# Eight modulation chunks of the first layer as scaled sums on ScalarE, GpSimd and VectorE instead of TensorE matmuls

## The chip, the core and the metric

The kernel runs on one core of a Trainium2 chip. The metric is the device time of one execution, in microseconds (us). Five engines of the core matter here, each with its own queue, worked off in order: TensorE (PE; its weight loads are listed apart as PEld), VectorE (DVE), ScalarE (ACT), GpSimd (POOL), and SyncE (SP), which here only issues DMA transfers. Engines wait for each other through semaphores. TensorE writes only to PSUM; tensors named z, zS, U, T, S and O lie there, all others used below in SBUF.

## The reference, cut to what matters

```python
def modulation(cond, w_ada, b_ada):
    m = jax.nn.silu(cond) @ w_ada + b_ada          # (1024) @ (1024, 6144)
    return [t[..., None, :] for t in jnp.split(m, 6, axis=-1)]
...
for i in range(DEPTH):                             # two layers
    sh1, sc1, g1, sh2, sc2, g2 = modulation(c, w_ada[i], b_ada[i])
    csh1, csc1, cg1, csh2, csc2, cg2 = modulation(c_ctx, w_ada[i], b_ada[i])
    h = modulate(rms_norm(x, norm1_g[i]), sh1, sc1)
    hc = modulate(rms_norm(ctx, norm1_g[i]), csh1, csc1)
    ...                                            # h @ w_in, mixers A, B and C
    x = x + g1 * (jnp.concatenate([out_a, out_b, out_c], axis=-1) @ w_out[i])
    x = x + g2 * conv_ffn(modulate(rms_norm(x, norm2_g[i]), sh2, sc2), ...)
    ...                                            # the same for ctx, unless last
```

There are 1024 latent tokens and 256 context tokens of width 1024, two layers. The modulation is a product of one vector per stream (latent with `c`, context with `c_ctx`) with a matrix of 1024 x 6144, cut by the kernel into 12 chunks of 512 columns. Chunks 0 to 3 (shift and scale of the first norm) are needed before the input projection. Chunks 4 to 11 (gate g1, then shift, scale and gate of the second half) are needed only from the output projection on.

## The kernel before

Tokens lie in 10 tiles of 128: tiles 0 to 7 latent, 8 and 9 context. The first layer normalises tiles in the order `al` = 8, 9, 0, 1, 2 and `be` = 3 to 7. `ipset` (L1042) runs the input projection block by block (`cb` 3, 2, 1, 0, each 512 columns), and for each block tile by tile in `inproj` (L415). One tile of one block is 24 matmuls of 128x128 on 128x512 (L132: three terms of high and low halves, eight slices of the depth). Behind them the tile's result `z` is copied by ScalarE to `zs` (L435), normed and rotated in `rms_rope` (L369: ScalarE squares, VectorE sums, GpSimd raises to the power -1/2 at L381, VectorE and GpSimd rotate at L382 to L394), transposed on TensorE (L400, PSUM tile `U`, one buffer) and written to DRAM. Weights come in units of 512 KB into a ring of three buffers (`raw` of pool `wr`), and are split into halves by ScalarE (L115) and VectorE (L109).

Between the projection blocks stand the differential attention `attn_c` (scores at L696 into `S`, running maximum at L496 on VectorE, exponent at L704 on ScalarE, mix at L710 on VectorE, transposes at L724, output at L729) and the window attention `attn_b` (L568 to L620, closing at L629 to L637). Then follow the output projection in `prep` (L130 with `oT`), the second norm, and the MLP.

The modulation chunks 4 to 11 are `modset` calls at the end of that list (`range(4, 8)` and `range(8, 12)` around the last `ipset`). `mod_chunk` (L134) loads a chunk as four quarters of 256 rows (512 KB each, into the same `raw` ring as the weights), multiplies each 128 rows by the padded condition columns `cpad` on TensorE (L143), both streams at once, copies the 512-wide result (L144), transposes it with four TensorE transposes (L147), and sums and adds the bias on VectorE (L149, L151). The second layer does its chunks in another manner, during the first layer's MLP: `mod_wide` (L153) scales the rows on ScalarE (L167, L170), adds them on GpSimd (L171), transposes within blocks of 32 on VectorE (L176), reduces (L177), and at the end `mod_sum` (L180) sums over the blocks with small matmuls (L187).

The order of instructions in each engine's queue is not that of the source. A scheduler sets it when the program is built, with the source order as priority, and lets later work go ahead where its inputs and buffers are ready. So the trace shows attention matmuls between the projection's, and the chunks between both.

Of the kernel before, what the change touches and what calls it, by code (L numbers as in the profile page):

```python
# [52 lines left out]
def trunk(ctx: ExitStack, tc: tile.TileContext, a: dict):  # L53
# [127 lines left out]

    def mod_sum(L, c0, c1, ns, mkps):

        ps = mkps()
        n = (c1 - c0) * 4 * ns
        for b in range(4):
            pe.matmul(ps[32 * b:32 * b + 32, 0:n], four, st["modr"][:, b, c0:c1, :, 0:ns].rearrange("p c m s -> p (c m) s"),  # L187
                      start=True, stop=True)
        dve.tensor_tensor(out=mods[:, L, 4 * c0:4 * c1, 0:ns], in0=ps[:, 0:n].rearrange("p (c s) -> p c s", s=ns),
                          in1=bcol[:, L, 4 * c0:4 * c1].unsqueeze(2).to_broadcast([P, 4 * (c1 - c0), ns]), op=ALU.add)  # L190
# [9 lines left out]
    def norm_front(src, mkps, mkbig, f=None, ss=None):  # L200

        ms = sm.tile([P, 2], F32, tag="nms", name="nms")
        if ss is None:
            sq = mkbig()
            act.activation(out=sq, in_=src, func=AF.Square)
            red = sm.tile([P, P], F32, tag="red", name="red", bufs=1)
            for w_ in (4, 2):
                dve.tensor_tensor(out=sq[:, 0:w_], in0=sq[:, 0:w_], in1=sq[:, w_:2 * w_], op=ALU.add)
            dve.tensor_tensor(out=red, in0=sq[:, 0], in1=sq[:, 1], op=ALU.add)
            ps = mkps()  # L210
            pe.transpose(ps[:, 0:P], red, ident)
# [5 lines left out]
        dg = sm.tile([P, P], F32, tag="dg", name="dg", bufs=2)  # L217
# [289 lines left out]
    def units_b(L, tiles, at, mkS, mkT, mkO):  # L507
# [11 lines left out]
        def unit(g):  # L519
# [76 lines left out]
            def outputs(hp, pp):  # L596
# [34 lines left out]
                ob = at.tile([P, 512], F32, tag="ob", name="ob", bufs=1)  # L631
                act.activation(out=ob[:np_], in_=po[:np_], func=AF.Copy)
                dve.tensor_tensor(out=ob[:np_], in0=bc[:np_], in1=ob[:np_], op=ALU.mult)
                st = at.tile([P, 2, 512], F32R, tag="stb", name="stb", bufs=1)
                st = [st[:, 0], st[:, 1]]
# [428 lines left out]
    ipset(0, al, (1,))  # L1064
# [206 lines left out]
```

## Time and profile before

| | before |
|---|---|
| median of three runs | 3282.14 us (3276.18 to 3285.51) |
| profiled execution | 3282.18 us |
| its span, first to last instruction | 3280.3 us |
| busy share PE, DVE, ACT, POOL | 94%, 71%, 53%, 27% |
| start of the output projection of the first layer | 469.6 us |
| start of its first MLP matmul | 601.6 us |

The work that the change touches lies in the first 605 us of the span. A busy engine is not an engine at its peak: a wait inside a matmul counts as busy. The trace lists one fp32 matmul of the source as two where it is done in two passes, as at L143 (128 in the trace for chunks 4 to 11) and L187. "PEclk" is the share of the TensorE clock that was granted.

### The profile page before, as it was taken

The page shows a single profiled execution, that of the slowest core. Times are in us where ns is not written, and L with a number is a line of the kernel's source. Part 1 is how long each engine was busy: PE and PEld are TensorE (multiplying, and loading weights), DVE is VectorE, ACT ScalarE, POOL GpSimd, SP SyncE. Part 2 cuts the span into 40 slices and gives each one's busy share as a digit, 9 for nine tenths or more (in the row PEclk, how much of TensorE's full clock was granted, in tenths as well). Part 3 has the DMA queues.
Part 4 walks back from the last instruction along what each step waited for, and adds up shares of the span by engine and source line. Part 5 has one row for each costly group of instructions (what it writes and reads, how often), then busy time and mean ns, then how long its engine had stood idle before and what let it go on. Part 6 is the DMA issues. An engine that isn't in the chain of part 4 may idle for free.

```text
span 3280.3 us, 54515 instructions
## 1 busy us (share of the span) xinstructions
PE 3072.3 (94%) x19503; PEld 2754.6 (84%) x19503; DVE 2330.4 (71%) x5306; ACT 1742.7 (53%) x3075; POOL 892.2 (27%) x1170
## 2 busy tenths in 40 slices
PE   6999988899999899999999899999898999999999
PEld 3777656798999898989999777777897799999998
DVE  4776765766878875878776678757786685666666
ACT  3554545656656653646444345567675564444443
POOL 1445301133223640128101144223240322231000
PEclk8999998899999999999999999999999999999999
DMA  8655796345543763378333656455754546434443
GB/s 265 193 161 173 205 273 165 91 125 144 135 120 100 232 178 113 103 209 242 93 106 108 173 132 175 139 166 141 180 147 131 134 114 204 122 101 137 138 119 104
DMA packets 754126, 499.52 MB, mean 152 GB/s; under 512 B 81480, under 2 KB 697792, under 8 KB 753856
## 3 DMA queue, kind: packets, MB, share of 16 engines
q1 hardware_dynamic: 753856, 496.03, 53.1%
q8 instruction: 155, 2.54, 0.3%
q14 instruction: 115, 0.94, 0.1%
HBM read 432.48 MB, written 63.44 MB: 151 GB/s over the span
## 4 chain that ended last, share of the span: by engine, by line
PE 64%; DVE 11%; DMA 8%; ACT 4%; POOL 3%; issue 3%; SPq 1%; ACTq 0%; POOLq 0%; DVEq 0%
PE z L130 32%; PE zS L130 11%; PE z L132 6%; PE O L620 2%; DVE wsp L109 2%; DMA raw<-in_w_up_dram 2%; DMA mraw<-in_w_ada_dram 2%; PE T L610 2%; PE O L729 2%; DVE ec L496 2%; PE S L696 1%; POOL mev L171 1%; POOL wsp L109 1%; PE zS L132 1%; PE T L724 1%
## 5 line engine op out<-in xcount | busy, mean ns | idle before, releaser
L130 PE MATMUL z<-h,wsp 128*128 128x386 f32 (+3 forms) x5280 | 872.1, 319 | 17.4 <-ACT wsp L115 5.7
L130 PEld LDWEIGHTS z<-h,wsp 128*128 128x128 f32 x5280 | 821.9, 190 | 31.6 <-issue 9.3
L115 ACT ACTIVATE wsp<-raw 128x1024 fp32r<-128x1024 f32 (+2 forms) x660 | 555.7, 845 | 423.7 <-PE z L130 185.2
L109 DVE TENSOR_TENSOR wsp<-raw,wsp 128x1024 fp32r<-128x1024 f32 (+2 forms) x516 | 562.6, 1092 | 108.2 <-ACT wsp L115 105.2
L130 PE MATMUL z<-g,wsp 128*128 128x386 f32 (+3 forms) x2640 | 457.0, 321 | 13.7 <-DVE t L862 4.7
L130 PEld LDWEIGHTS z<-g,wsp 128*128 128x128 f32 x2640 | 415.6, 190 | 28.3 <-issue 8.8
L132 PE MATMUL z<-wsp,h 128*128 128x512 f32 x1584 | 406.2, 403 | 16.6 <-ACT h L233 5.3
L109 POOL TENSOR_TENSOR wsp<-raw,wsp 128x128 fp32r<-128x128 f32 x528 | 258.5, 522 | 426.6 <-ACT wsp L115 358.4
L132 PEld LDWEIGHTS z<-wsp,h 128*128 128x128 f32 x1584 | 293.5, 192 | 83.3 <-ACT zs L435 6.4
L130 PE MATMUL zS<-h,wsp 128*128 128x386 f32 (+1 forms) x2112 | 333.4, 313 | 9.8 <-DVE wsp L109 3.4
L130 PEld LDWEIGHTS zS<-h,wsp 128*128 128x128 f32 x2112 | 318.0, 190 | 12.6 <-DVE wsp L109 4.2
L855 ACT ACTIVATE t<-z,cw 128x386 f32<-128x386 f32 (+3 forms) x220 | 137.9, 627 | 186.3 <-PE z L130 184.9
L859 DVE SCALAR_TENSOR_TENSOR t<-z,cw,t 128x255 f32<-128x255 f32 (+3 forms) x264 | 132.4, 502 | 145.2 <-ACT t L855 144.5
L704 ACT ACTIVATE ec<-ec,nmc 128x1280 f32<-128x1280 f32 (+1 forms) x144 | 182.3, 1266 | 72.8 <-DVE ec L496 70.7
L171 POOL TENSOR_TENSOR mev<-mev,mtr 128x512 f32<-128x512 f32 x112 | 175.7, 1582 | 122.6 <-ACT mtr L170 119.7
L496 DVE TENSOR_SCALAR_CACHE_REDUCE ec<-S,nmc 128x512 f32<-128x512 f32 (+1 forms) x256 | 173.5, 678 | 41.1 <-PE S L696 36.7
L130 PE MATMUL z<-oT,wsp 128*128 128x384 f32 (+2 forms) x1056 | 198.9, 337 | 3.9 <-DMA oT<-o_s 3.7
L887 DVE SCALAR_TENSOR_TENSOR xg<-z,mods,xg 128x384 f32<-128x384 f32 (+5 forms) x288 | 140.1, 501 | 85.4 <-PE z L130 84.2
L130 PE MATMUL zS<-g,wsp 128*128 128x386 f32 (+1 forms) x1056 | 182.8, 317 | 9.7 <-DVE wsp L109 3.0
L130 PEld LDWEIGHTS z<-oT,wsp 128*128 128x128 f32 x1056 | 178.3, 190 | 12.0 <-issue 4.3
L381 POOL TENSOR_TENSOR rs<-ss,cst 128x8 f32<-128x8 f32 (+1 forms) x76 | 115.5, 1520 | 225.7 <-DVE ss L379 146.1
L696 PE MATMUL S<-Kc,qc 128*128 128x512 f32 (+1 forms) x400 | 143.6, 401 | 35.0 <-DVE ec L496 27.2
(248 smaller groups left out, 4678.6 us busy)
## 6 DMA issues: line engine op xcount, KB each, us to landing
raw<-in_w_up_dram SPq DMA_DIRECT2D x264, 512.0 KB
mraw<-in_w_ada_dram SPq DMA_DIRECT2D x96, 512.0 KB
raw<-in_w_down_dram SPq DMA_DIRECT2D x192, 256.0 KB
Kc<-qk_s SPq DMA_DIRECT2D x96, 320.0 KB
raw<-in_w_in_dram SPq DMA_DIRECT2D x52, 512.0 KB
raw<-in_w_out_dram SPq DMA_DIRECT2D x48, 512.0 KB
raw<-in_w_down_dram SPq DMA_DIRECT2D x104, 192.0 KB
qk_s<-st SPq DMA_DIRECT2D x18, 512.0 KB
```

The lines of the kernel that those rows point to most:

```text
L109: eng.tensor_tensor(out=lo, in0=src, in1=hi.bitcast(F32), op=ALU.subtract)
L115: act.activation(out=hl[:, 0], in_=raw, func=AF.Copy)
L130: pe.matmul(ps, w(i, k), h(j, k), start=s, stop=e)
L132: pe.matmul(ps, h(i, k), w(j, k), start=s, stop=e)
L171: pool.tensor_tensor(out=acc[s], in0=acc[s], in1=pr, op=ALU.add)
L381: pool.tensor_tensor(out=rs[:, :ns], in0=ss[:, 1, :ns], in1=mhalf[:, :ns], op=ALU.pow)
L496: dve.tensor_scalar(out=neg, in0=s_ap, scalar1=-1.0, scalar2=init, op0=ALU.mult, op1=ALU.min, accum_out=acc)
L696: pe.matmul(S[:, b * w_:b * w_ + w_], q[:, m, ti * P:ti * P + P], K[m][:, o:o + w_], start=True, stop=True)
L704: act.activation(out=es[m][:, :nk], in_=es[m][:, :nk], func=AF.Exp, scale=-1.0, bias=acc[m], accum_out=l1[:, m, ti:ti + 1])
L855: act.activation(out=t[:, o:o + n], in_=ps[:, :n], func=AF.Identity, scale=cw[:, L, 1, ft:ft + 1], bias=cw[:, L, 3, ft:ft + 1])
L859: dve.scalar_tensor_tensor(out=t[:, o + b + 1:o + e], in0=ps[:, b:e - 1], scalar=cw[:, L, 0, ft:ft + 1], in1=t[:, o + b + 1:o + e], op0=AL ...
L887: dve.scalar_tensor_tensor(out=xs, in0=ps[:, b + o0:b + o1], scalar=mods[:, L, 40 + ct, s:s + 1], in1=xs, op0=ALU.mult, op1=ALU.add)
```

## The change

Chunks 4 to 11 of the first layer go through a new function `mod_mix`. A quarter is loaded as before. The latent stream (s = 0) is scaled on ScalarE into a temporary and added to its sum on GpSimd; the context stream (s = 1) is multiplied and added in one VectorE instruction. After the fourth quarter VectorE transposes and reduces both sums, four small matmuls sum over the blocks, and VectorE adds the bias. A quarter is called before each tile of the projection blocks (`between=modq`) and before each head of one attention call, 32 quarters in all, and the two `modset` calls go.

Three smaller edits free SBUF: the second norm's last VectorE addition writes into its input instead of a tile `red`; `dg` has one buffer instead of two; and `ob` of the window attention is the second half of the output tile `stb`, which GpSimd then overwrites in place. `prep_loads` makes `oT` before `xg`.

```diff
+    def mod_mix(L, ch, mkraw, mkacc, mktr, mkps):
+        acc = [mkacc() for _ in range(2)]
+        def quarter(j):
+            raw = mkraw()
+            sp.dma_start(out=raw, in_=a["w_ada"][L, j * 256:j * 256 + 256, ch * 512:ch * 512 + 512]
+                         .rearrange("(k p) c -> p k c", p=P))
+            for k in range(2):
+                c0, c1 = (cpad[:, 2 * j + k, s:s + 1] for s in range(2))
+                if j == 0 and k == 0:
+                    act.activation(out=acc[0], in_=raw[:, k], func=AF.Identity, scale=c0)
+                    dve.tensor_scalar(out=acc[1], in0=raw[:, k], scalar1=c1, scalar2=None, op0=ALU.mult)
+                else:
+                    pr = mktr()
+                    act.activation(out=pr, in_=raw[:, k], func=AF.Identity, scale=c0)
+                    pool.tensor_tensor(out=acc[0], in0=acc[0], in1=pr, op=ALU.add)
+                    dve.scalar_tensor_tensor(out=acc[1], in0=raw[:, k], scalar=c1, in1=acc[1], op0=ALU.mult,
+                                             op1=ALU.add)
+            if j < 3:
+                return
+            mr = sm.tile([P, 4, 4, 2], F32, tag="mr", name="mr", bufs=1)
+            for s in range(2):
+                tr = mktr()
+                dve.transpose(tr, acc[s])
+                dve.tensor_reduce(out=mr[:, :, :, s].rearrange("p b m -> p m b"),
+                                  in_=tr.rearrange("p (m b j) -> p m b j", b=4, j=32), axis=AX.X, op=ALU.add)
+            ps = mkps()
+            for b in range(4):
+                pe.matmul(ps[32 * b:32 * b + 32, 0:8], four, mr[:, b].rearrange("p m s -> p (m s)"), start=True, stop=True)
+            dve.tensor_tensor(out=mods[:, L, 4 * ch:4 * ch + 4], ...)
...
-            for w_ in (4, 2):
+            for w_ in (4, 2, 1):
                 dve.tensor_tensor(out=sq[:, 0:w_], in0=sq[:, 0:w_], in1=sq[:, w_:2 * w_], op=ALU.add)
-            dve.tensor_tensor(out=red, in0=sq[:, 0], in1=sq[:, 1], op=ALU.add)
...
-        dg = sm.tile([P, P], F32, tag="dg", name="dg", bufs=2)
+        dg = sm.tile([P, P], F32, tag="dg", name="dg", bufs=1)
...
+                st = at.tile([P, 2, 512], F32R, tag="stb", name="stb", bufs=1)
+                st = [st[:, 0], st[:, 1]]
+                ob = st[1].bitcast(F32)
...
-    ipset(0, al, (1,))
+    def modq(i=None):
+        n = mq["n"]
+        if n == 32:
+            return
+        if n % 4 == 0:
+            mq["q"] = mod_mix(0, 4 + n // 4, lambda: wr.tile([P, 2, 512], F32, tag="raw", name="mraw", bufs=3),
+                              lambda: wk.tile([P, 512], F32, tag="mev", name="mev", bufs=2),
+                              lambda: wk.tile([P, 512], F32, tag="sq", name="mtr", bufs=wb["sq"]), mkU)
+        mq["q"](n % 4)
+        mq["n"] += 1
+
+    ipset(0, al, (1,), between=modq)
...
-    ipset(0, al, (0,))
+    ipset(0, al, (0,), between=modq)
     st["wd"] = 1
-    ipset(0, be, (3, 2))
+    ipset(0, be, (3, 2), between=modq)
     for hd in range(4):
+        modq()
         attn_c(0, hd, [(0, 1)], at, mkS, mkT, mkO)
-    ipset(0, be, (1,))
-    modset(0, range(4, 8), wk, "kn", wr, "raw", 3, mkz, mkU)
-    ipset(0, be, (0,))
-    modset(0, range(8, 12), wk, "kn", wr, "raw", 3, mkz, mkU)
+    ipset(0, be, (1, 0), between=modq)
```

The temporaries take the tag `sq`, whose three buffers `rms_rope` uses too, and the quarters the `raw` ring of three.

How the built queues moved is shown at three places. In the changed program the lines are 33 higher from `norm_front` on and 34 higher inside the attention (L400 is L433, L696 is L730). On TensorE, in the differential attention of tiles 0 and 1 before (`zs` and `wst` belong to projection block 0 of tiles 3 to 7):

```order
L143 MATMUL z<-mraw,cpad 32x512 x2
L696 MATMUL S<-Kc,qc 128x512
L143 MATMUL z<-mraw,cpad 32x512 x2
L400 MATMUL U<-cst,zs 128x128 x2
L143 MATMUL z<-mraw,cpad 32x512 x2
L696 MATMUL S<-Kc,qc 128x512
L478 MATMUL U<-zs,wst 128x64 x4
```

and in the same attention in the changed program:

```order
L730 MATMUL S<-Kc,qc 128x512
L730 MATMUL S<-Kc,qc 128x256 x2
L132 MATMUL z<-wsp,h 128x512 x12
L730 MATMUL S<-Kc,qc 128x512
L211 MATMUL U<-mr,four 32x8 x4
L132 MATMUL z<-wsp,h 128x512 x44
L730 MATMUL S<-Kc,qc 128x512
```

The chunk's matmuls are gone there, four small ones stand for a whole chunk, and projection matmuls fill what lies between the scores.

On GpSimd, in projection block 1 of the first five tiles (q of the window attention), before:

```order
L381 TENSOR_TENSOR rs<-ss,cst 128x8
L390 TENSOR_TENSOR r_1489<-kn,tab 128x16x16 x2
L381 TENSOR_TENSOR rs<-ss,cst 128x8
L390 TENSOR_TENSOR r_1541<-kn,tab 128x16x16 x2
L381 TENSOR_TENSOR rs<-ss,cst 128x8
```

and now:

```order
L414 TENSOR_TENSOR rs<-ss,cst 128x8
L423 TENSOR_TENSOR r_1509<-kn,tab 128x16x16 x2
L198 TENSOR_TENSOR mev<-mev,mtr 128x512 x2
L414 TENSOR_TENSOR rs<-ss,cst 128x8
L423 TENSOR_TENSOR r_1571<-kn,tab 128x16x16 x2
L198 TENSOR_TENSOR mev<-mev,mtr 128x512 x2
```

Two additions of a quarter stand now between the two steps of one tile and those of the next.

On VectorE, in projection block 2 of tiles 3 to 7, the end of a chunk and the start of the next in the changed program (`stc` is attention output, `ko` and `ss` belong to `rms_rope`):

```order
L199 SCALAR_TENSOR_TENSOR mev<-mraw,cpad,mev 128x512 x2
L415 TENSOR_TENSOR ko<-zs,rs 128x256
L425 TENSOR_TENSOR ko<-ko,tab 128x256
L427 TENSOR_TENSOR ko<-ko,r_3447 128x256
L206 STREAM_TRANSPOSE mtr<-mev 128x512 x2
L800 SCALAR_TENSOR_TENSOR stc<-T,sg,stc 128x128
L207 TENSOR_REDUCE mr<-mtr 128x4x4 x2
L194 TENSOR_SCALAR mev<-mraw,cpad 128x512
L411 TENSOR_REDUCE ss<-sq 128x2
```

None of these `mev`, `mtr` and `mr` rows stood there before; they come between the steps of the projection tiles.

The 32 loads of `w_ada` are still issued by SP. The first of them now stands where projection block 2 of `al` is in work, the last just ahead of the first load of `w_out`; before, all 32 stood between the first loads of the window attention and that load.

More of the change, by code (lines that the diff above doesn't have):

```diff
@@ L180, in mod_wide @@
         return quarter
+    def mod_mix(L, ch, mkraw, mkacc, mktr, mkps):
[26 more added lines that the diff above has]
+                pe.matmul(ps[32 * b:32 * b + 32, 0:8], four, mr[:, b].rearrange("p m s -> p (m s)"), start=True, stop=True)
+            dve.tensor_tensor(out=mods[:, L, 4 * ch:4 * ch + 4], in0=ps[:, 0:8].rearrange("p (m s) -> p m s", s=2),
+                              in1=bcol[:, L, 4 * ch:4 * ch + 4].unsqueeze(2).to_broadcast([P, 4, 2]), op=ALU.add)
+        return quarter
     def mod_sum(L, c0, c1, ns, mkps):
@@ L205, in norm_front @@
             act.activation(out=sq, in_=src, func=AF.Square)
-            red = sm.tile([P, P], F32, tag="red", name="red", bufs=1)
-            for w_ in (4, 2):
+            for w_ in (4, 2, 1):
                 dve.tensor_tensor(out=sq[:, 0:w_], in0=sq[:, 0:w_], in1=sq[:, w_:2 * w_], op=ALU.add)
-            dve.tensor_tensor(out=red, in0=sq[:, 0], in1=sq[:, 1], op=ALU.add)
             ps = mkps()
-            pe.transpose(ps[:, 0:P], red, ident)
+            pe.transpose(ps[:, 0:P], sq[:, 0], ident)
             ss = ms[:, 0:1]
@@ L630, in outputs @@
                               start=True, stop=True)
-                ob = at.tile([P, 512], F32, tag="ob", name="ob", bufs=1)
+                st = at.tile([P, 2, 512], F32R, tag="stb", name="stb", bufs=1)
+                st = [st[:, 0], st[:, 1]]
+                ob = st[1].bitcast(F32)
                 act.activation(out=ob[:np_], in_=po[:np_], func=AF.Copy)
                 dve.tensor_tensor(out=ob[:np_], in0=bc[:np_], in1=ob[:np_], op=ALU.mult)
-                st = at.tile([P, 2, 512], F32R, tag="stb", name="stb", bufs=1)
-                st = [st[:, 0], st[:, 1]]
                 act.activation(out=st[0][:np_], in_=ob[:np_], func=AF.Copy)
@@ L786, in prep_loads @@
         wd = G["W"]
+        oT = p.tile([P, 2, KT, wd], F32R, tag="h", name="oT", bufs=1)
         xg = p.tile([P, KT, wd], F32, tag="xg", name="xg", bufs=1)
-        oT = p.tile([P, 2, KT, wd], F32R, tag="h", name="oT", bufs=1)
         def load(k):
@@ L1062, in trunk @@
     at = mkpool("at0", 2, "left")
-    ipset(0, al, (1,))
+    mq = {"n": 0}
+    def modq(i=None):
[9 more added lines that the diff above has]
+    ipset(0, al, (1,), between=modq)
     for hd in range(4):
@@ L1068, in trunk @@
         attn_b(0, t, at, mkS, mkT, mkO)
-    ipset(0, al, (0,))
+    ipset(0, al, (0,), between=modq)
     st["wd"] = 1
-    ipset(0, be, (3, 2))
+    ipset(0, be, (3, 2), between=modq)
     for hd in range(4):
+        modq()
         attn_c(0, hd, [(0, 1)], at, mkS, mkT, mkO)
-    ipset(0, be, (1,))
-    modset(0, range(4, 8), wk, "kn", wr, "raw", 3, mkz, mkU)
-    ipset(0, be, (0,))
-    modset(0, range(8, 12), wk, "kn", wr, "raw", 3, mkz, mkU)
+    ipset(0, be, (1, 0), between=modq)
+    assert mq["n"] == 32
     mod_scale(0, 1)
```

## The prediction

> **What bounds the kernel now.** I read the page first, then the stretch that the change touches, cut into windows, then what TensorE waits for there.
>
> ```profile
> PE 3072.3 (94%) x19503; PEld 2754.6 (84%) x19503; DVE 2330.4 (71%) x5306; ACT 1742.7 (53%) x3075; POOL 892.2 (27%) x1170
> ```
>
> Over the whole span TensorE is the engine with least slack. The windows show whether that also holds where the chunks are. Columns are start and end, length, busy us of PE, PEld, DVE, ACT and POOL, the granted clock, DMA share and GB/s:
>
> ```profile
> 160.00:200.00 40.00, 36.14 (x179) 28.26 (x179) 33.15 (x75) 21.15 (x43) 22.51 (x20) 1.00 0.50 145
> 280.00:320.00 40.00, 40.00 (x223) 27.23 (x222) 24.75 (x96) 19.49 (x50) 25.19 (x36) 1.00 0.54 158
> 440.00:480.00 40.00, 31.70 (x215) 20.52 (x216) 26.91 (x91) 18.52 (x34) 2.59 (x4) 0.91 0.88 266
> 560.00:605.00 45.00, 27.29 (x115) 18.89 (x116) 36.41 (x95) 31.95 (x62) 12.47 (x8) 0.62 0.48 129
> ...
> 140.00:605.00 465.00, 407.86 (x2302) 299.21 (x2301) 314.63 (x951) 247.16 (x513) 148.85 (x172) 0.94 0.64 185
> 140.00:470.00 330.00, 300.13 (x1655) 213.02 (x1654) 232.91 (x709) 170.19 (x366) 124.03 (x145) 0.98 0.67 196
> 1083.00:1200.00 117.00, 102.68 (x562) 99.33 (x561) 100.13 (x122) 82.40 (x133) 89.62 (x57) 0.93 0.65 205
> ```
>
> From 140 to 470 us TensorE is 91% busy (300.13 of 330) and VectorE 71%. At 280 to 320 TensorE is full. At 440 to 480 it is not, and the DMA engines are 88% busy: that is where quarters of `w_ada` arrive. The last row is for later: the second layer's chunks, in the new manner, with the chip's busiest VectorE stretch of that length that I found, 100.13 of 117, or **0.856**.
>
> **What the change removes.** TensorE's time on chunks 4 to 11, all of it between 300 and 500 us (rows of L143, then L147), and its idle time ahead of L143 (waits of TensorE from 140 to 605 us: total, times, longest):
>
> ```profile
> 300.00:500.00 200.00, 32.38 (x128) 4.53 (x128) 0.95 0.82 241
> ...
> 300.00:500.00 200.00, 5.18 (x32) 3.63 (x32) 0.95 0.82 241
> ...
> PE S L696 <- DVE ec L496: 9.7, 11, 4.0
> PE z L143 <- DMA mraw<-in_w_ada_dram: 8.9, 6, 2.2
> ```
>
> In place of 37.6 us of TensorE come 32 small matmuls. The nearest rows are those of the second layer's block sum, where eight in the source are sixteen in the trace:
>
> ```profile
> L187 PEld LDWEIGHTS U<-modr,four x16: 106/108/109, 1382.3 to 1577.4; 128*32 128x32 f32 x16
> L187 PE MATMUL U<-modr,four x16: 196/206/217, 1382.3 to 1577.5; 128*32 128x32 f32 x16
> ```
>
> So 64 in the trace. Following each other at the pace of their weight loads they take 64 x 0.106 = 6.8 us; the bounds are nothing and 64 x 0.206 = 13.2. Net TensorE loses 37.6 - 6.8 = **30.8 us**, and with the 8.9 us of waits that go, the ceiling of the gain is **39.7 us**.
>
> **What it adds.** VectorE's durations are taken from the chain of work, where an instruction counts without its overlap with the one before (start us, us, what):
>
> ```profile
> 192.49 0.60 DVE zs L462
> 345.22 0.60 DVE mev L144
> ...
> 1107.72 0.62 DVE mtr L176
> 1110.11 0.57 DVE modr L177
> ...
> L149 DVE TENSOR_REDUCE mods<-U x12: 180/187/193, 13.1 to 463.3; 128x8 f32<-128x32 f32 x12
> ...
> L151 DVE TENSOR_TENSOR mods<-mods,bcol x12: 161/167/1254, 13.3 to 467.3; 128x8 f32<-128x8 f32 x12
> ```
>
> L462 is a scalar-tensor-tensor of 128x512 with both tensors in SBUF, like the new one: 56 x 0.60 = 33.6. The eight first products have no row; I take the same 0.60 as the upper end, half of it as the lower, and the middle: 8 x 0.45 = 3.6. Sixteen transposes, 9.9, and sixteen reductions, 9.1. Eight closing additions at L151's 0.167, 1.3. That is 57.5. Off go eight copies (4.8), eight L149 (1.5) and eight L151 (1.3): net **+50 us of VectorE**. ScalarE and GpSimd take these (count, then busy us, mean ns):
>
> ```profile
> L170 ACT ACTIVATE mtr<-mraw,cpad 128x512 f32<-128x512 f32 x112 | 78.6, 717 | 30.3 <-POOL mev L171 24.1 <-DMA mraw<-in_w_ada_dram 4.0 <-DVE modr L177 1.9
> ...
> L171 POOL TENSOR_TENSOR mev<-mev,mtr 128x512 f32<-128x512 f32 x112 | 175.7, 1582 | 122.6 <-ACT mtr L170 119.7 <-DMA gt<-in_b_qnorm_dram 0.3
> ```
>
> ScalarE: 64 x 0.717 = 46 us, on 247 of 465; it stays at 63%. GpSimd: 56 x 1.582 = 89 us, on 149 of 465; 51%. Neither is full on the mean. ScalarE's wait for GpSimd (24.1 us over 112) would be half that; its 172 us of slack hold it.
>
> **What VectorE loses beside GpSimd.** The two streams of a quarter run side by side, and the trace shows that they disturb each other:
>
> ```profile
> 585.31 2.36 POOL L109 TENSOR_TENSOR h<-nb,h 128x1024 fp32r<-128x1024 f32 x1 [7.39 <-ACT h L233]
> ...
> 585.51 2.31 DVE L209 TENSOR_TENSOR red<-nb 128x128 f32<-128x128 f32 x1
> ```
>
> A VectorE addition of 128 elements, begun beside a GpSimd subtraction, ends 0.15 us after it. How often that happens beside L171 is read from the same instructions with its 112 additions (1083 to 1571 us) and without (1600 to 1800):
>
> ```profile
> L109 DVE TENSOR_TENSOR wsp<-raw,wsp 128x1024 fp32r<-128x1024 f32 x66 | 86.9, 1317 | 19.6 <-ACT wsp L115 19.6
> L109 DVE TENSOR_TENSOR wsp<-raw,wsp 128x512 fp32r<-128x512 f32 x41 | 37.6, 918 | 0.3
> L870 DVE TENSOR_TENSOR t<-t,th 128x516 f32<-128x516 f32 x8 | 11.0, 1381 | 0.1
> ...
> L109 DVE TENSOR_TENSOR wsp<-raw,wsp 128x1024 fp32r<-128x1024 f32 x25 | 30.6, 1224 | 2.5 <-ACT wsp L115 2.4
> L109 DVE TENSOR_TENSOR wsp<-raw,wsp 128x512 fp32r<-128x512 f32 x16 | 11.0, 689 | 0.7 <-ACT wsp L115 0.4
> L870 DVE TENSOR_TENSOR t<-t,th 128x516 f32<-128x516 f32 x11 | 7.6, 690 | 0.1
> ```
>
> The excess is 66 x 0.093 + 41 x 0.229 + 8 x 0.691 = 6.1 + 9.4 + 5.5 = 21 us over 112 additions, 0.19 each, and other shapes there have no clean row. For 56 that is at least 10.5 us; at most every addition stops VectorE for its whole length, 89. The new work is itself of the kind that is held up and VectorE is fuller here, but its attention work at L496 reads scores from PSUM, so I stay near the row and take **18 us**.
>
> The Trainium skill ("SBUF — State Buffer", section "SBUF: two separate sides") says that GpSimd and VectorE share one pair of SBUF ports as an exclusive lock: a VectorE instruction with two SBUF inputs and a GpSimd one that reads SBUF exclude each other for a whole instruction. The 2.31 us above agrees; the excess of 0.19 us per addition shows that the price is far under a whole one of 1.58 where VectorE has other work. It speaks against this change, and the strict case is the last rival.
>
> **Edits costed at nothing.** `red`: the same additions, one shape. `dg` with one buffer: the next norm's `dg` must wait for the matmul at L220, but that tile's squares, sums and power come between. `ob` inside `stb`: ScalarE's copy at L632 must now wait until the stores of the previous unit have landed, with all later ScalarE work behind it, and TensorE behind PSUM `O`. The chain has the closings at L629 and landings of DMAs:
>
> ```profile
> 314.66 1.01 PE T L629 x4
> ...
> 337.89 1.01 PE T L629 x4
> 370.62 1.01 PE T L629 x4
> 416.46 10.52 DMA Kc<-qk_s
> ...
> 500.84 2.45 DMA o_s<-stc
> ```
>
> Closings are 23 us and more apart, landings take 2 to 11, so they are hidden; uncovered, it is 11 us once.
>
> **The moved loads.** The 32 loads keep their count and size, and meet a DMA share of 0.50 at 160 us, not 0.88. On SP they now stand ahead of stores and table loads of the projection; one that waits for a `raw` buffer holds these back. In the MLP 48 such loads waited:
>
> ```profile
> SPq L161 <- ACT mtr L170: 42.8, 22, 3.5
> ```
>
> 0.9 us each, so 29 us for 32. I take nothing, since four `zs` and three `kn` buffers lie between a tile's matmuls and its stores; if one such wait of 3.5 us shows at each of the six projection calls that hold quarters, it is 21 us, about the price of the pile-up below.
>
> **The forecast.** With 30.8 us less of TensorE and 68 us more of VectorE, VectorE is the tighter engine: 314.63 + 50 + 18 = 383 us, where TensorE has 408 - 31 = 377. If VectorE gets as full as in the fullest row, the stretch from 140 to 605 us takes 383 / 0.856 = 447 us instead of 465: **-18 us**. The profiled execution took 3282.18 us (span 3280.3), the median of the runs is 3282.14, so both give 3264. Stalls of 10.5 to 25 us give 3255 to 3272.
>
> **Rivals.**
> *TensorE alone sets the end.* VectorE runs ahead in the attention, so its load is spread; the whole ceiling is had: 3282 - 40 = 3242. For it: at 280 to 320 TensorE is full with VectorE at 62%. Against it: in the row at 1083 the same work left TensorE idle for 14 us of 117.
>
> *GpSimd sets the pace of the projection tiles.* One tile of block 1 needs on GpSimd a power and two rotations, and now two additions:
>
> ```profile
> L381 POOL TENSOR_TENSOR rs<-ss,cst 128x8 f32<-128x8 f32 x30 | 53.1, 1770 | 43.5 <-DVE ss L379 40.8 <-DVE ls L590 2.7
> ...
> L390 POOL TENSOR_TENSOR r<-kn,tab 128x256 f32<-128x256 f32 x20 | 17.2, 878 | 12.8 <-DVE kn L382 9.2 <-DVE ls L590 3.6
> ...
> 388.26 5.51 PE z L132 x24
> ```
>
> 1.77 + 2 x 0.878 + 2 x 1.582 = 6.7 us, against 5.5 for the tile's 24 matmuls: 1.2 us late for each of ten such tiles, 12 us, that come off the gain: 3276. It decides from the point where no attention stands between the tiles. This is my case for no change.
>
> *VectorE piles up where the chunks were put.* The quarters are ordered between 140 and 470 us, where attention and rotation already use VectorE; at 160 to 200 it is at 83% before the change. If its work can't be moved out of that part, it takes (232.91 + 68) / 0.856 = 352 us instead of 330: +22, **3304**, slower. It decides from 0.856 x 330 = 282 us of VectorE, and the sum of 301 is beyond. Against it: 480 to 605 us has attention whose VectorE work can be done earlier or later.
>
> *Every GpSimd addition stops VectorE.* Then 314.63 + 50 + 89 = 454, over 0.856 is 530 us: +65, 3347. The Trainium skill's lock, taken strictly, gives this.
>
> *The chunks don't move* is out: the queue rows show them moved.
>
> **How the numbers follow.** TensorE alone 0.16 (3242); forecast 0.40 (3264); GpSimd's pace 0.20 (3276); pile-up 0.20 (3304); strict stop 0.04. Under 0.3%, 9.8 us, a measurement can't tell a change from none. The first two are faster, with a little of the second inside the bound and of the third beyond it: faster 0.56. Same 0.21, slower 0.23. The range takes in the ceiling with the small matmuls at nothing and a little clock won, 3238, and the pile-up, 3306; what is left out is the strict stop and the tails, under 2 in 10.
>
> **What would show it.** Right: no `mraw` wait of TensorE after 140 us; VectorE at 82 to 88% from 140 to the first MLP matmul, which starts near 584 instead of 601.6; new VectorE additions of 0.60 to 0.69 us with a tail to 2 us; L171's like at 1.3 to 1.6 us. Pile-up: TensorE waits ending in `wsp`, `st` or `ec` of VectorE, and the output projection starting later than 469.6. GpSimd's pace: waits for `rs` L381 above today's. Wrong altogether: a changed time beyond 700 us, where nothing was moved but `dg`, `red` and `ob`.

## The result, and the profile after

| | before | after |
|---|---|---|
| median of four runs each | 3283.45 us (3276.18 to 3285.51) | 3342.09 us (3337.74 to 3344.61) |
| ratio, 95% interval | | 1.0178 (1.0161 to 1.0195): slower |
| span of the profiled execution | 3280.3 us | 3339.2 us |
| start of the output projection, first layer | 469.6 us | 546.8 us |
| start of its first MLP matmul (L130, `z<-h,wsp`) | 601.6 us | 647.7 us |
| 1584th of the matmuls at L130 and L132 (in the first layer's MLP) | 710.5 us | 753.1 us |
| 7920th of them (end of the first layer's MLP) | 1845.3 us | 1888.3 us |
| 8976th of them (second layer, before its MLP) | 2250.6 us | 2309.3 us |

The change costs 58.9 us of span, in two places: 46.1 us before the first MLP matmul, where the chunks are, and 15.7 us between the last two rows, where no chunk is. The first layer's MLP between gives back about 3.

Page of the changed kernel, busy us and share of the span of each engine:

```profile
PE 3085.9 (92%) x19407; PEld 2775.1 (83%) x19407; DVE 2417.0 (72%) x5386; ACT 1781.4 (53%) x3139; POOL 972.9 (29%) x1226
```

TensorE lost the chunks and yet is 13.6 us *more* busy than before. The windows of the changed kernel, with the prediction's columns, say where:

```profile
160.00:200.00 40.00, 26.05 (x104) 19.00 (x105) 33.88 (x44) 18.30 (x28) 24.85 (x19) 0.74 0.55 164
280.00:320.00 40.00, 29.75 (x135) 22.17 (x134) 29.93 (x76) 19.99 (x47) 23.16 (x25) 0.79 0.59 175
440.00:480.00 40.00, 33.57 (x183) 26.01 (x182) 37.13 (x75) 22.36 (x38) 18.64 (x16) 0.96 0.63 193
140.00:648.00 508.00, 409.05 (x2191) 313.42 (x2190) 401.20 (x1023) 285.69 (x577) 235.51 (x232) 0.84 0.60 169
```

At 160 to 200 us TensorE went from 36.14 busy us at clock 1.00 to 26.05 at 0.74; at 280 to 320 from full to 29.75. From 140 us to the first MLP matmul VectorE has 401.20 us, and the same stretch of the kernel before (to 602 us) has this sum:

```profile
sum 462.00, PE 405.29 PEld 297.59 DVE 312.49 ACT 245.34 POOL 146.42; mean PE 405.29 PEld 297.59 DVE 312.49 ACT 245.34 POOL 146.42
```

So VectorE has 88.7 us more, but fills only 401.20 of 508, 0.79. No engine is full. The groups of VectorE show part of the 88.7, first before, then after (count, busy us, mean ns, idle time ahead and what ended it):

```profile
L392 DVE TENSOR_TENSOR kn<-kn,tab 128x512 f32<-128x512 f32 x10 | 7.8, 776 | 3.0 <-POOL r L390 2.9
L394 DVE TENSOR_TENSOR kn<-kn,r 128x512 f32<-128x512 f32 x10 | 7.2, 725 | 0.0
```

```profile
L199 DVE SCALAR_TENSOR_TENSOR mev<-mraw,cpad,mev 128x512 f32<-128x512 f32 x51 | 44.9, 881 | 2.9 <-DMA mraw<-in_w_ada_dram 2.6
...
L425 DVE TENSOR_TENSOR kn<-kn,tab 128x512 f32<-128x512 f32 x10 | 14.8, 1478 | 2.3 <-POOL r L423 2.2
...
L427 DVE TENSOR_TENSOR kn<-kn,r 128x512 f32<-128x512 f32 x10 | 12.8, 1282 | 0.2
```

The two rotation instructions of a `q` tile (L392 and L394, now L425 and L427) take nearly twice as long, for the same data. The timeline of the changed kernel at a `q` tile shows how (start, us, engine, line, tile, idle time ahead and its releaser):

```profile
169.60 0.68 DVE L425 TENSOR_TENSOR kn<-kn,tab 128x512 f32<-128x512 f32 x1
169.65 3.44 POOL L198 TENSOR_TENSOR mev<-mev,mtr 128x512 f32<-128x512 f32 x2 [0.38 <-ACT mtr L197]
...
170.32 1.63 DVE L427 TENSOR_TENSOR kn<-kn,r 128x512 f32<-128x512 f32 x1
...
172.10 1.09 PE L433 MATMUL U<-cst,kn 128*128 128x128 f32 x4 [3.77 <-DVE kn L427]
...
177.10 3.85 POOL L198 TENSOR_TENSOR mev<-mev,mtr 128x512 f32<-128x512 f32 x2
178.07 1.75 DVE L425 TENSOR_TENSOR kn<-kn,tab 128x512 f32<-128x512 f32 x1
```

L425 takes 0.68 us where it starts ahead of a GpSimd addition and 1.75 beside one; L427, begun beside one, takes 1.63, and TensorE waits 3.77 us behind it. The Trainium skill ("SBUF — State Buffer", section "SBUF: two separate sides") has GpSimd and VectorE lock a shared pair of ports for a whole instruction. The trace agrees: taken singly, L427 at 170.32, L425 at 178.07 and L427 at 179.86 each end 0.55 us after the addition beside which they began, so nearly all of their clean 0.68 us comes behind it.

What TensorE waits for, 140 to 648 us after (total, times, longest):

```profile
PE S L730 <- DVE ec L529: 15.0, 20, 2.6
PE T L758 <- ACT ec L759: 9.8, 6, 4.7
PE z L132 <- ACT wsp L115: 6.7, 4, 3.3
PE U L433 <- DVE st L109: 5.7, 2, 2.9
PE T L797 <- DVE o L793: 5.7, 3, 2.5
```

The `mraw` waits are gone; in their place are many of other kinds, behind VectorE and ScalarE alike.

### The profile page after: what moved, and what is told of

The parts are those of the page before. It is cut to its first block, busy times and chain, and to the rows that moved or that the text cites. A ratio compares the mean times of both kernels' runs of the same rounds, so it can differ in the third digit from the quotient of the medians.

```text
span 3339.2 us, 54628 instructions
## 1 busy us (share of the span) xinstructions
PE 3085.9 (92%) x19407; PEld 2775.1 (83%) x19407; DVE 2417.0 (72%) x5386; ACT 1781.4 (53%) x3139; POOL 972.9 (29%) x1226
## 5 line engine op out<-in xcount | busy, mean ns | idle before, releaser
L130 PE MATMUL z<-h,wsp 128*128 128x386 f32 (+3 forms) x5280 | 872.7, 319 | 20.0 <-DVE t L896 6.5
L130 PEld LDWEIGHTS z<-h,wsp 128*128 128x128 f32 x5280 | 823.6, 191 | 34.8 <-issue 12.1
L130 PE MATMUL z<-g,wsp 128*128 128x386 f32 (+3 forms) x2640 | 455.5, 321 | 11.6 <-DVE t L896 3.6
L132 PE MATMUL z<-wsp,h 128*128 128x512 f32 x1584 | 420.3, 414 | 26.4 <-ACT h L266 8.8
L130 PEld LDWEIGHTS z<-g,wsp 128*128 128x128 f32 x2640 | 414.8, 190 | 25.6 <-issue 6.7
L132 PEld LDWEIGHTS z<-wsp,h 128*128 128x128 f32 x1584 | 304.2, 199 | 101.2 <-ACT wsp L115 10.5
L130 PE MATMUL zS<-h,wsp 128*128 128x386 f32 (+1 forms) x2112 | 334.0, 313 | 9.3 <-DVE t L896 4.0
L130 PEld LDWEIGHTS zS<-h,wsp 128*128 128x128 f32 x2112 | 318.8, 191 | 11.6 <-ACT wsp L115 6.2
L130 PE MATMUL z<-oT,wsp 128*128 128x384 f32 (+2 forms) x1056 | 196.8, 335 | 6.2 <-DMA oT<-o_s 6.1
L130 PE MATMUL zS<-g,wsp 128*128 128x386 f32 (+1 forms) x1056 | 182.4, 317 | 7.9 <-ACT wsp L115 2.8
L130 PEld LDWEIGHTS z<-oT,wsp 128*128 128x128 f32 x1056 | 176.3, 188 | 15.1 <-ACT x L493 4.0
L730 PE MATMUL S<-Kc,qc 128*128 128x512 f32 (+1 forms) x400 | 147.5, 410 | 39.2 <-DVE ec L529 32.6
```

The source lines that it names most:

```text
L130: pe.matmul(ps, w(i, k), h(j, k), start=s, stop=e)
L132: pe.matmul(ps, h(i, k), w(j, k), start=s, stop=e)
L730: pe.matmul(S[:, b * w_:b * w_ + w_], q[:, m, ti * P:ti * P + P], K[m][:, o:o + w_], start=True, stop=True)
```

## The experiments

The mark used below is the start of the first MLP matmul, beside 601.6 us before. A single execution can't tell a few us: the same kernel (`ob` alone) was profiled twice and had the mark at 585.0 and 582.0, the end of the span at 3266.5 and 3272.2. Most rows of the table are one execution each. Kernels that leave work out serve to price it; they compute something else.

| kernel | first MLP matmul | against before | span |
|---|---|---|---|
| no chunks 4 to 11 at all | 569.6 | -32.0 | 3245.5 |
| change, products on ScalarE narrow, no adds, no multiply-adds | 588.0 | -13.6 | 3273.1 |
| change, no adds, no multiply-adds | 605.1 | +3.5 | 3302.4 |
| change, no GpSimd adds | 622.5 | +20.9 | 3323.1 |
| change, no VectorE multiply-adds | 626.1 | +24.5 | 3324.6 |
| change, both streams on VectorE | 622.7 | +21.1 | 3310.6 |
| change, quarters at the old place | 640.2 | +38.6 | 3327.0 |
| change without the exchange in `prep_loads` | 647.5 | +45.9 | 3335.7 |
| change | 647.7 | +46.1 | 3339.2 |
| chunks on TensorE, at the new place | 609.4 | +7.8 | 3282.5 |
| the four edits alone | 601.1 | -0.5 | 3286.1 |
| `red` and `dg` alone | 599.9 | -1.7 | 3284.3 |
| exchange (`oT` ahead of `xg`) alone | 597.7 | -3.9 | 3277.6 |
| `ob` alone (two profiles) | 585.0, 582.0 | -16.6, -19.6 | 3266.5, 3272.2 |
| `ob`, chunks 10 and 11 later | 594.2 | -7.4 | 3275.3 |
| chunks 10 and 11 in the MLP | 592.0 | -9.6 | 3413.1 |

**The four edits alone**, on the kernel before:

```diff
-            red = sm.tile([P, P], F32, tag="red", name="red", bufs=1)
-            for w_ in (4, 2):
+            for w_ in (4, 2, 1):
...
-            dve.tensor_tensor(out=red, in0=sq[:, 0], in1=sq[:, 1], op=ALU.add)
...
-        dg = sm.tile([P, P], F32, tag="dg", name="dg", bufs=2)
+        dg = sm.tile([P, P], F32, tag="dg", name="dg", bufs=1)
...
-                ob = at.tile([P, 512], F32, tag="ob", name="ob", bufs=1)
...
+                ob = st[1].bitcast(F32)
...
+        oT = p.tile([P, 2, KT, wd], F32R, tag="h", name="oT", bufs=1)
         xg = p.tile([P, KT, wd], F32, tag="xg", name="xg", bufs=1)
-        oT = p.tile([P, 2, KT, wd], F32R, tag="h", name="oT", bufs=1)
```

> The kernel before with only the three SBUF edits (red gone, dg with one buffer, ob inside stb, oT made before xg); chunks 4 to 11 stay on TensorE. Theory: the changed kernel lost about 42 us up to its first MLP and 16 us more in the second layer's projections and attention (1850 to 2250 us), where no chunk stands; the edits cause the 16. Then no shift up to 1850 us and 12 to 18 us by the end: 3294 to 3302. Rival: the 16 us come from how the second layer's queues happened to be ordered behind the chunk work; then within 5 us of the kernel before.

3289.48 us against 3280.66, ratio 1.0029 (1.0017 to 1.0041). Between the two theories: against before, -0.5 us at the mark, +3.3 at the 7920th matmul and +5.9 at the 8976th.

**The quarters at the old place**, all edits kept:

```diff
-    ipset(0, al, (1,), between=modq)
+    ipset(0, al, (1,))
...
-    ipset(0, be, (1, 0), between=modq)
+    ipset(0, be, (1,))
+    for _ in range(16):
+        modq()
+    ipset(0, be, (0,))
+    for _ in range(16):
+        modq()
```

> The changed kernel with the same quarters called where the modset calls stood (16 behind block 1 of tiles 3 to 7, 16 behind block 0). Theory that the place decides (early quarters stand in the q and k tiles' norm chains): first MLP matmul at 602 to 622 us instead of 648, end at 3295 to 3315. Theory that the operations decide, wherever they stand: first MLP matmul at 635 or later, end above 3330.

3329.65 us, ratio 1.0152 (1.0135 to 1.0169). The first MLP matmul is 38.6 us late, of the change's 46.1, and the 1584th matmul 45.7, where the change has 42.5. So the place is not the cause of most of it: the loss follows the operations.

**One stream left out at a time**:

```diff
-                    pool.tensor_tensor(out=acc[0], in0=acc[0], in1=pr, op=ALU.add)
```

> The changed kernel without the 56 GpSimd additions: the latent stream's sums of chunks 4 to 11 hold only the first of eight products. Theory that GpSimd's additions (in the tiles' chains, and holding VectorE up) cost most of the loss: first MLP matmul at 600 to 622 us. Theory that VectorE's own 50 us cost it: 632 to 645. The second layer keeps its 14 to 18 us either way.

```diff
-                    dve.scalar_tensor_tensor(out=acc[1], in0=raw[:, k], scalar=c1, in1=acc[1], op0=ALU.mult,
-                                             op1=ALU.add)
```

> The changed kernel without the 56 VectorE multiply-adds of 0.60 us: the context stream's sums hold only the first product. Theory that VectorE's own work decides: first MLP matmul at 605 to 620 us (34 us and their hold-ups gone). Theory that GpSimd decides: 630 or later.

3324.94 and 3326.35 us, the marks at 622.5 and 626.1: each takes away about half of the 46.1. The first mark lies 0.5 us above its range for GpSimd, the second between its two ranges: neither stream is the whole loss. From the 1584th matmul to the end they lose 22 and 21 us, more than the 14 to 18 expected. VectorE's groups without GpSimd's additions (same stretch):

```profile
L198 DVE SCALAR_TENSOR_TENSOR mev<-mraw,cpad,mev 128x512 f32<-128x512 f32 x51 | 39.0, 764 | 7.6 <-DMA mraw<-in_w_ada_dram 7.3
...
L426 DVE TENSOR_TENSOR kn<-kn,r 128x512 f32<-128x512 f32 x10 | 6.8, 685 | 0.1
L424 DVE TENSOR_TENSOR kn<-kn,tab 128x512 f32<-128x512 f32 x10 | 6.8, 682 | 3.2 <-POOL r L422 3.1
```

and without VectorE's multiply-adds:

```profile
L423 DVE TENSOR_TENSOR kn<-kn,tab 128x512 f32<-128x512 f32 x10 | 15.7, 1572 | 7.5 <-POOL r L421 7.5
L425 DVE TENSOR_TENSOR kn<-kn,r 128x512 f32<-128x512 f32 x10 | 12.6, 1257 | 0.1
```

The rotation falls back to 0.68 us when GpSimd's additions go, and stays at 1.26 to 1.57 when VectorE's own new work goes. So the hold-ups come from GpSimd's additions. How much they are in all, VectorE's sums to the mark tell; first without the additions (with them it was 401.20), then without the multiply-adds:

```profile
sum 482.00, PE 394.95 PEld 303.40 DVE 353.28 ACT 279.65 POOL 153.99; mean PE 394.95 PEld 303.40 DVE 353.28 ACT 279.65 POOL 153.99
```

```profile
sum 486.00, PE 399.17 PEld 304.43 DVE 357.82 ACT 276.82 POOL 222.45; mean PE 399.17 PEld 304.43 DVE 357.82 ACT 276.82 POOL 222.45
```

The additions, which run on GpSimd, raise VectorE's busy time by 47.9 us (353.28 to 401.20). Without the multiply-adds they raise it by 40.0: from 317.78, the sum of the kernel that has neither (below), to 357.82. VectorE's own work is the same in each pair, but for some instructions near the mark that fall inside the longer stretch.

**The ceiling, and the rest taken apart.** First the kernel before without the chunks:

```diff
-    modset(0, range(4, 8), wk, "kn", wr, "raw", 3, mkz, mkU)
...
-    modset(0, range(8, 12), wk, "kn", wr, "raw", 3, mkz, mkU)
```

> The kernel before without chunks 4 to 11 at all (no loads, no matmuls, no transposes; the chunks stay zero). It measures the ceiling of any move of this work. Theory 'the prediction's ceiling': TensorE was the bound, so all 39.7 us of matmuls, transposes and waits on mraw come off: first MLP matmul near 562 (601.6 before), end near 3241. Rival 'the stage has a second bound close by': VectorE and its chains with TensorE carry the stage as soon as the chunks leave; first MLP matmul at 575 to 595 and end 3255 to 3275, with a lower granted clock in 140 to 560 us.

3247.3 us, first MLP matmul 32.0 us earlier. That lies between the theory (39.7; 46.5 for this kernel, since the 39.7 has 6.8 us of small matmuls already taken off, which are not here either) and the rival (7 to 27, with a lower clock: it is 0.92, before 0.94). Doing nothing in place of this work wins 32 us here, 35 over the span (30 by the time of the kernel before that ran beside it, 3277.05).

Then the change without additions and multiply-adds, that is with the two diffs above together:

> The changed kernel without the 56 adds on GpSimd and without the 56 multiply-adds on VectorE; loads, ScalarE's products, first products, transposes, reductions and the small matmuls stay. Theory 'VectorE pile-up' (its own work and its hold-ups beside GpSimd add up): the first MLP matmul comes at 585 to 605 (647.7 in the changed kernel, 622.5 and 626.1 with one of the two left out). Rival 'order and ring' (weights that come late behind the quarters' loads, quarters' products on ScalarE ahead of the projection's): still 615 or later.

3304.14 us, the mark at 605.1, at the very end of the range. But then the two removed operations are not the whole cost: 35.5 us still lie between this kernel and the one without chunks. So ScalarE's products, which the prediction had for nothing, were cut to 16 columns, in that kernel:

```diff
-                    act.activation(out=pr, in_=raw[:, k], func=AF.Identity, scale=c0)
+                    act.activation(out=pr[:, 0:16], in_=raw[:, k, 0:16], func=AF.Identity, scale=c0)
```

> The changed kernel without the adds on GpSimd and the multiply-adds on VectorE, and with each of ScalarE's 56 products cut to 16 of 512 columns (same places in the queues, same waits, less time). Without the cut the first MLP matmul came 33 us behind the kernel that has no chunks at all (1584th matmul +3.2 against -31.6). Theory 'ScalarE's 38 us of products are on the path' (its copies release TensorE's operands and VectorE's inputs): that mark moves to between -10 and -20. Rival 'places and waits' (the loads between the weights on SP's queue and in the ring, VectorE's transposes and reductions): it stays between -3 and +4.

The 1584th matmul came at -15.0 us: the theory's middle. The sums from 140 us to the first MLP matmul of three kernels, no chunks, narrow products, full products:

```profile
sum 430.00, PE 374.10 PEld 292.22 DVE 302.65 ACT 244.36 POOL 151.66; mean PE 374.10 PEld 292.22 DVE 302.65 ACT 244.36 POOL 151.66
```

```profile
sum 448.00, PE 384.40 PEld 299.59 DVE 318.65 ACT 257.69 POOL 145.86; mean PE 384.40 PEld 299.59 DVE 318.65 ACT 257.69 POOL 145.86
```

```profile
sum 465.00, PE 391.86 PEld 301.76 DVE 317.78 ACT 278.18 POOL 147.25; mean PE 391.86 PEld 301.76 DVE 317.78 ACT 278.18 POOL 147.25
```

From the second to the third ScalarE gets 20.5 us more work, and the stretch is 17.1 us longer (marks 588.0 and 605.1), though ScalarE is busy only 58 to 60% of it.

A rival to all these steps is order. The scheduler orders each kernel's queues anew, and of the 2534 TensorE instructions up to the mark at most 2051 stand in the same sequence in the last two kernels (2134 and 2171 where the kernel with full products is set beside those that have one stream of the sums back). With the same operations in another order the mark moved by up to 20 us in kernels further on (`ob` alone; with `red` and `dg` twice as many instructions changed places, and it moved by 1.7 us). So a single step of 17 to 21 us is not proved to be its operation's price. The whole is beyond order's reach as seen here: 78.1 us from no chunks (569.6) to the change (647.7).

**Both streams on VectorE**:

```diff
-                    act.activation(out=acc[0], in_=raw[:, k], func=AF.Identity, scale=c0)
+                    dve.tensor_scalar(out=acc[0], in0=raw[:, k], scalar1=c0, scalar2=None, op0=ALU.mult)
...
-                    pr = mktr()
-                    act.activation(out=pr, in_=raw[:, k], func=AF.Identity, scale=c0)
-                    pool.tensor_tensor(out=acc[0], in0=acc[0], in1=pr, op=ALU.add)
-                    dve.scalar_tensor_tensor(out=acc[1], in0=raw[:, k], scalar=c1, in1=acc[1], op0=ALU.mult,
-                                             op1=ALU.add)
+                    for c_, a_ in ((c0, acc[0]), (c1, acc[1])):
+                        dve.scalar_tensor_tensor(out=a_, in0=raw[:, k], scalar=c_, in1=a_, op0=ALU.mult, op1=ALU.add)
```

> The changed kernel with both streams on VectorE: no products on ScalarE and no adds on GpSimd; VectorE gets 56 more multiply-adds (0.60 us each, 34 us) and one more first product for each chunk, and loses its hold-ups beside GpSimd (some 38 us more of them than before, by durations above the lower quartile). Theory 'VectorE pile-up': the two cancel, first MLP matmul 635 to 655, end 3325 to 3345. Rival 'GpSimd's place in the chain' (rs and r behind the adds on GpSimd's queue, which the hold-ups don't count): first MLP matmul below 630.

3312.51 us, the mark at 622.7: the rival's side, and a miss for "VectorE's load alone". Its window:

```profile
140.00:623.00 483.00, 393.87 (x2192) 305.33 (x2191) 397.03 (x1090) 245.82 (x511) 159.88 (x176) 0.88 0.63 176
```

VectorE is as busy as in the change (397.03 and 401.20 us), and the stretch is 25 us shorter. So VectorE's sum alone does not set the time. Prices per operation come closer: 56 multiply-adds cost 17.4 us (no adds against neither: 622.5 - 605.1), so 112 of them on the narrow-product kernel would give 588.0 + 34.8 = 622.8. Measured: 622.7. That they meet to 0.1 us is partly chance: the narrow products, which this kernel lacks, are not taken off in that sum, its eight further first products are not added, and single executions differ by 3 us.

**The chunks on TensorE, at the new place**, one whole chunk after every fourth of the 32 places:

```diff
+    def modc(i=None):
+        n = mq["n"]
+        mq["n"] += 1
+        if n % 4 == 3 and n < 32:
+            modset(0, (4 + n // 4,), wk, "kn", wr, "raw", 3, mkz, mkU)
...
+    ipset(0, al, (1,), between=modc)
```

> The kernel before with each of chunks 4 to 11 still on TensorE, whole, but called after every fourth of the changed kernel's 32 places: loads and place as in the change, operations as before. Theory 'the operations decide': first MLP matmul at 595 to 605, end 3276 to 3288. Rival 'place and ring decide': 615 or later, end above 3295.

3284.26 us in one run, within the theory's range for the end, span 2.2 us over before. The mark, at 609.4, lies between the two ranges, 4.4 us above the theory's and 5.6 below the rival's. Loads that come early and share the weights' ring cost some 8 us here, order included (whole chunks; the change's quarters come one by one).

**Which edit.** Each alone on the kernel before: `red` with `dg`, then `ob`, then the exchange; and the change without the exchange.

> The kernel before with two of the edits: red gone (the last sum stays in sq) and dg with one buffer. All four edits cost 6 to 9 us, all behind the 7920th matmul. Theory 'a later normalisation waits for sq or dg': 6 to 9 us there again, with TensorE waiting some 8 us on h in 1845 to 2260 us. Rival 'ob': within 2 us of before there.

> The kernel before with ob in the second half of stb, nothing else. Theory 'ob' (the next pair's copy waits for the store of the last): 5 to 9 us behind the 7920th matmul and up to 3 us in the first layer. Rival 'red and dg': within 2 us of before.

> The kernel before with only oT allocated ahead of xg in prep_loads. Theory 'the exchange costs': the 1584th matmul 10 to 16 us later than before. Rival 'it costs nothing by itself and only undoes what ob gained, by another order': within 3 us of before at that mark.

> The changed kernel with xg allocated ahead of oT again. Theory 'the exchange costs': the 1584th matmul at 738 to 743 (753.1 in the changed kernel). Rival 'the operations cost, in any order': within 4 us of the changed kernel at that mark.

`red` and `dg` gave 3286.16 us (before 3281.21). Behind the 7920th matmul they lost 1.6 us up to the 8976th, so the time is in the rival's range, though the waits that the theory names are there; the four edits together, too, lost only 2.6 us of their 5.9 behind that mark. Waits of TensorE on `h` in the second layer's projections, first the change, then this kernel; before, L233's `h` cost 0.7 us there:

```profile
PE z L132 <- ACT h L266: 4.8, 2, 3.0
PE zS L132 <- ACT h L266: 4.2, 1, 4.2
```

```profile
PE z L132 <- ACT h L231: 4.4, 2, 2.7
...
PE zS L132 <- ACT h L231: 3.7, 1, 3.7
```

So the waits on `h`, 8 to 9 us, come with `red` and `dg`. They don't fix the loss: the change with quarters at the old place has them too (8.8 us) and loses 1.0 us between the 1584th matmul and the end, the change 16.3, the change without additions, with the same 8.8 us, 22.2.

`ob` alone was a surprise: 3268.35 us, the opposite of what was expected of it. The exchange alone costs nothing (3279.34), and the change without it is where the change is (the 1584th matmul at 753.2 and 753.1). Up to the mark it leaves the order of TensorE, VectorE, ScalarE and GpSimd as it was, so its -3.9 us there is the spread of single executions. The first layer's -0.5 us of all four edits is not a sum of theirs (-1.7, -18, -3.9). `ob` alone moves some 190 of TensorE's instructions up to the mark, `red` and `dg` some 380, and with all four edits TensorE's order is that of `red` and `dg` alone: the gain of `ob` is gone beside them.

**Faster than both?** `ob` alone, five rounds:

> The kernel before with ob in the second half of stb, nothing else, timed in five rounds (one look gave 3268.35 us, with the 1056th matmul 17.4 us earlier). Theory 'the edit moves the second layer-1 pair of the b heads behind the projections and shortens the stage by 16 us': 3265 to 3271, ratio 0.995 to 0.997. Rival 'that one execution was by chance': within 0.1% of before.

3273.17 us against 3284.84, ratio **0.9968** (0.9957 to 0.9979): faster than both kernels. The ratio is in the expected range, the time 2 us above it. The mechanism that the expectation names was not shown; the instruction order differs at many places from the window attention on.

The same with chunks 10 and 11 on TensorE, but later:

```diff
-    modset(0, range(8, 12), wk, "kn", wr, "raw", 3, mkz, mkU)
+    modset(0, range(8, 10), wk, "kn", wr, "raw", 3, mkz, mkU)
...
     x1 = prep(0, G0[0], X1, M)
+    modset(0, (10, 11), at, "ob", wr, "raw", 3, mkz, mkU)
```

> The kernel before with the ob edit, chunks 4 to 9 as they were and chunks 10 and 11 still on TensorE but called after the first w_out stage is set up, where TensorE is busy 23 of 40 us (560 to 600 us) and waits for the attention and the normalisation. Theory 'TensorE's work is free where it waits': 2 to 7 us less than ob alone: 3262 to 3268. Rival 'its loads and its PSUM bank delay the chain that TensorE waits for': 3268 or more.

3279.08 us, ratio 0.9985 (0.9974 to 0.9995), but slower than `ob` alone: the rival's side.

And the kernel before with chunks 10 and 11 in the wide form in the first MLP:

```diff
-    modset(0, range(8, 12), wk, "kn", wr, "raw", 3, mkz, mkU)
+    modset(0, range(8, 10), wk, "kn", wr, "raw", 3, mkz, mkU)
...
+        for n in range(2 * f, min(2 * f + 2, 8)):
+            if n % 4 == 0:
+                st["q"] = modwide(0, 10 + n // 4, 2, mo)
+            st["q"](n % 4)
+        if f == 4:
+            mod_sum(0, 10, 12, 2, mkU)
...
+    at.release()
+    mo = mkpool("mo2", 1, "left")
+    st.update(modr=mo.tile([P, 4, 12, 4, 2], F32, name="modr"))
```

> The kernel before, with chunks 4 to 9 on TensorE as they were and only chunks 10 and 11 (needed first by the first w_down block) off it, by the existing wide form on ScalarE and GpSimd, two quarters at each of the first four w_up blocks of the first MLP. There VectorE is busy 70 to 80 of 108 us and GpSimd 24, where the projections have VectorE nearly full. Theory 'the same move pays where VectorE has room': a quarter of the 30 us that all eight chunks are worth comes off ahead of the MLP, and 0 to 4 us are lost in it: 3274 to 3280 beside 3281, ratio 0.9975 to 0.9995. Rival 'hold-ups in the MLP cost as much': 3281 to 3290.

3417.95 us, ratio 1.0417 (1.0402 to 1.0431): both theories missed it. The loads of these chunks up to 900 us, four of the eight (L161; duration of an issue, first and last start):

```profile
L161 SPq DMA_DIRECT2D mraw<-in_w_ada_dram x4: 368/452/546, 888.4 to 895.3; - x4
```

The MLP began at 592.0, but its loads for chunks 10 and 11 went out from 888 us on. Their tiles stand where the attention pool `at` was, attention work fills that stretch (TensorE waits at L696, with `ec` of L496), and I read the wait as one for memory that comes free only when it ends; that was not tried by itself. The experiment says nothing on the price of the move itself.

## Why the prediction was wrong

The forecast was 3264 us, -18; measured were 3342. The steps, one by one:

- **TensorE is the bound at 140 to 470 us, ceiling 39.7 us.** Held in kind. Without the chunks the stretch is 32.0 us shorter, where TensorE's 37.6 us and the 8.9 us of waits make 46.5; the ceiling was 14 us too high. The small matmuls, sized at 6.8 us, took 2.04.
- **VectorE's own new work, +50 us.** Undersized: a multiply-add took 0.731 to 1.844 us, median 0.748, not the 0.60 of L462's row, and 0.764 on the mean without GpSimd's additions. That is 9 us for 56. The row gave L462 without its overlap with the instruction before; its own records are 0.67 to 0.69.
- **18 us of hold-ups beside GpSimd.** Undersized by more than half: 40.0 and 47.9 us in the two pairs of kernels that differ in the additions alone. The row it was drawn from was an MLP, whose VectorE work was held up by 0.19 us per addition; in the projection the additions fall on the rotations, which have two inputs in SBUF: those of a `q` tile took 1478 and 1282 ns on the mean with the additions, 682 and 685 without.
- **ScalarE +46 us and GpSimd +89 us at nothing, since neither is full.** This is the step that failed, with the next one, which is its other side. Widening ScalarE's products from 16 columns to 512 lengthens the stretch by 17.1 us, with ScalarE busy 58% of it. GpSimd's additions cost 21.0 us where the multiply-adds are left out (626.1 against 605.1) and 25.2 where they stay (647.7 against 622.5); part of that is VectorE held up, which the prediction did count.
- **The stretch takes VectorE's sum over 0.856.** Failed with it. VectorE's sum came to 401.20 us instead of 383, which over 0.856 would make 469 us instead of 447; the other 39 us of the 508 are the fill, 0.79. And two kernels with nearly the same VectorE sum (397 and 401 us) were 25 us apart: the longer one has ScalarE's and GpSimd's new work, the shorter has not. The stretch is no engine's sum. My reading, argued from the waits and not tried by itself: a tile's work passes TensorE, ScalarE, VectorE, GpSimd, VectorE and TensorE in turn, and what any of them does in between makes the next later.
- **Edits at nothing.** Right for the first layer; wrong behind 700 us, which the prediction gave as the sign that it was wrong altogether. The change lost 16.3 us between the 1584th matmul and the end.
- **Moved loads at nothing.** Some 8 us with the chunks on TensorE at the new place, below the 21 named.
- **The range's lower end.** It was to take in the ceiling with the small matmuls at nothing, but 3282 - 46.5 is 3236, not 3238.

In one sum, from the marks: -32.0 for the work off TensorE; +18.4 for loads, first products, transposes, reductions, the narrow products and the edits; +17.1 for the rest of the products on ScalarE; +17.4 for the multiply-adds; +21.0 for the additions, and 4.2 more since these two meet: +46.1. The total is measured; the split is by single executions in differing orders, and each term is rough by some 10 us, an estimate from how far `ob`, `red` with `dg`, and the chunks at the new place moved the mark (-18, -1.7, +7.8).

Of the rivals, *pile-up* had the right signs (output projection 77 us later, waits ending in `wsp`, `st`, `ec`) and too small a price, +22, since it too counted VectorE alone. *GpSimd's pace* was wrong on its sign: VectorE's waits for `rs`, 15.5 us before up to the mark, are 8.2 after. *Every addition stops VectorE* has the nearest number, 3347, by accident: hold-ups were 40 to 48 us, not 89.

Left open: the 16 us behind the 1584th matmul, of which the waits on `h` are 9 at most; which of the moved instructions gives `ob` alone its gain; and TensorE's clock. TensorE was rid of 37.6 us and given 2.04, but its busy time in the stretch went up by 3.8 us, at a clock of 0.84 instead of 0.94, with 423 ns instead of 402 for an L132 matmul. Whether slow matmuls only filled waits or lengthened the stretch wasn't tried.

## What to carry to other kernels

Don't take an engine at 55% for free where its instructions stand between two steps of a chain that others wait for: price work moved to it by a run that leaves it out, not by its slack. Here a microsecond of added work cost roughly 0.8 for ScalarE (17.1 of 20.5), 0.4 for VectorE (17.4 of 56 x 0.764) and 0.25 for GpSimd (21.0 of 83.8). Before moving work off the bound, leave it out altogether in one run: here that showed 32 us to win, against three kinds of added work at 17 to 21 each and 18 for the rest. Measure small edits apart from the change they make room for; the small edit that gained lay hidden in a change that lost. And where a scheduler orders the queues, compare the orders before calling a difference of 10 or 20 us the price of an operation.

## What the hardware showed that was not expected

- TensorE's granted clock fell with its waits: from 1.00 to 0.74 at 160 to 200 us, where in the changed kernel it waits 3.3 to 4.9 us at a time. Taking the chunks off it does little to the clock by itself: without them, and with nothing in their place, it was 0.97 there and 0.92 over the stretch (0.94 before, 0.84 in the changed kernel):

```profile
160.00:200.00 40.00, 36.47 (x175) 28.79 (x176) 33.13 (x82) 21.91 (x46) 23.50 (x20) 0.97 0.49 138
...
140.00:570.00 430.00, 374.10 (x2121) 292.22 (x2120) 302.65 (x917) 244.36 (x508) 151.66 (x170) 0.92 0.58 160
```

  The Trainium skill ("TensorE: Matmul & The Clock Gate", section "Part 1: The HAM clock gate (the 'warmup' mystery)") gives an idle window of about 3.4 us for the half rate; the periods of half rate in the changed kernel's trace up to 660 us last 3.4 us or a multiple of it.
- GpSimd's 56 additions cost VectorE 40 to 48 us of busy time with the same work of its own, by the two pairs of kernels.
- A 128x512 scalar-tensor-tensor that scales by a column of SBUF and adds to its second tensor (L199) took 0.764 us on the mean without GpSimd's additions, where L462, which adds a constant and multiplies, also into its second tensor, took 0.67 to 0.69.
